# A gradient product on one core: all visits in a new order, and the last one split into 256 and 128 columns

## The chip, the core and the metric

The kernel runs on one core of a Trainium2 chip. A core has a matrix engine (TensorE, PE in the profile; its weight loads are shown apart, as PEld), VectorE (DVE), ScalarE (ACT), GpSimd (POOL) and SyncE (SP), each with its own queue of instructions, and 16 DMA engines which SP, ACT and POOL can give transfers to. Operands lie in SBUF, sums of TensorE in the eight banks of PSUM. The metric is the time of one execution on the device, in microseconds (us).

## What is computed

```python
# input: (16, 512, 1024) float32, grad_output: (16, 512, 768) float32
grad_weight = np.einsum('bmk,bmn->kn', input, grad_output)   # (1024, 768)
```

Batch and m are summed together: it is one product X^T G with X of 8192 x 1024 and G of 8192 x 768. The kernel rounds both to bf16 and sums in float32.

## The kernel before

**Blocks.** The output is cut into quarters: two halves of k (512 rows) by two halves of n (384 columns, LEFT and RIGHT). Each quarter has four row blocks q of 128. The quarters are called A (first k half, LEFT), B (first, RIGHT), C (second, LEFT), D (second, RIGHT). One matmul takes 128 rows of m as its contraction, 128 columns of X as weights, and 384 columns of G: every matmul is 128 by 128 by 384.

**Eight slabs plain, 28 pairs with seven products.** The first 1024 rows of m are eight slabs of 128 rows; each takes the four products A, B, C, D for every q. The other rows come as 28 pairs of 128 rows, each a 2 by 2 by 2 block product done with seven multiplications instead of eight (Winograd's form): streams A, B, C and 1, 5, 6, 7. Their operands are sums of halves of X and G, made by VectorE (`sum_x`, `sum_g`, lines 184 to 198, six instructions a pair). At the end the streams are joined: A gets 1, 6 gets 1, 7 gets 6, C gets 7, B gets 5, D is 5 minus 7, with D's own slabs folded in earlier (`SHARED`, and closings written with k). In all: 4 q x (3 x 36 + 8 + 4 x 28) = 912 matmuls.

**Visits.** There are 32 sums (8 streams x 4 q) and eight PSUM banks, so a sum visits a bank for a few matmuls, is evacuated to SBUF and comes back later. Three sums (A0, A1, A2) stay resident in banks 5 to 7 until near the end. Everything TensorE, VectorE, ScalarE and GpSimd do is written out as one list of tokens, `PLAN`, walked in order by the loop at the end of the function; each engine gets its instructions in exactly that order:

- `C0@2.1` opens bank 2 for C0 and does one matmul; `C0.1` goes on with one more; `@R` opens a resident bank (`multiply`, matmul at line 331).
- `fC2@0` has ScalarE copy C2's partial sum from SBUF into bank 0, so that the next visit adds onto it (`fill`, line 309; a trailing s takes it from an aside slot; two banks joined by + split it at column 256).
- `cC0` closes a visit by a ScalarE copy to SBUF (line 356), `vC0` by VectorE: a plain copy (line 376), an add onto the partial sum (378), or at the very end the join of two streams (364, 366, 371). `kC0` is the fold of D (360).
- `x0.4`, `g1.4` are VectorE's sums for pair 4. `r0` to `r4` are roundings of the first slabs to bf16: r0 is the RIGHT half of the first slab of G (VectorE), r1 and r2 halves of the second slab of X (VectorE), r3 and r4 the rest of it (ScalarE).
- `qA0` has GpSimd join two streams in SBUF (line 388) and stores the block; `pA3` joins ahead of the last visit ("prepared").

**Queues.** The first slabs come in float32 by SP and ACT (lines 128 to 131) and are rounded on chip; all other loads are cast to bf16 by GpSimd's DMA queue (lines 153 to 160), in order, into eleven buffers for pairs. Stores (line 291) go out on SP in the order of the tokens; the first HALVED of them are cut in two. Ahead of the first real matmul TensorE does 17 matmuls on constants, to the bank that A2 uses later (line 136).

Of the kernel before, what the change touches and what calls it, by code (L numbers as in the profile page):

```python
# [9 lines left out]
P = 128  # L10
# [4 lines left out]
    "C0@2.1 A0@R.1 r0 r1 r3 B1@1.1 r2 A2@R.1 r4 A1@R.1 vB1 A1.1 D3@4.2 A0.1 C0.1 D0@3.1 B2@0.1 cC0 B2.1 D0.1 "  # L15
    "fB1@1 A2.1 B3@2.2 cD3 B1.2 B3.1 D2@4.1 cB1 D2.1 vB3 D2.1 D0.1 A0.1 C1@2.3 C2@1.4 A1.2 cC2 B2.1 C1.1 B2.1 "
    "D2.1 cC1 D1@1.2 vD2 D1.1 fD3@2 D1.1 A2.2 cD0 vD1 B0@4.1 D3.2 A3@3.2 cD3 A3.2 B0.2 vA3 B0.1 C3@1.4 B2.2 "
    "B1@3.1 B0.1 cB2 B0.1 A1.2 cB0 D2@0.2 A0.3 D0@2.3 C3.2 A2.1 C0@4.1 vC3 C0.3 B1.2 B3@1.5 B1.1 D0.1 C0.1 vB1 "
    "C0.1 A0.2 vB3 D0.1 fD3@3 D2.2 vC0 fC3@1 A2.3 vD0 fD1@4 D3.3 vD2 D3.1 D1.1 g0.4 D1.1 fC1@0 D1.2 C3.1 fA3@2 "
    "g1.4 C3.1 C1.1 vD1 cD3 C1.3 kC3 fC2@3 A3.2 g2.4 A3.1 fB2@1 A3.1 x0.4 A3.1 C2.2 cA3 C2.1 x1.4 C2.2 A2.1 "  # L20
    "x2.4 10@2.1 cC2 A0.1 C1.1 v10 12@4.1 60@3.1 cC1 B2.1 g0.5 B2.1 c12 B2.1 61@0.1 g1.5 c60 62@2.1 B0@4.1 vB2 "
    "B0.1 c61 B0.1 11@3.1 c62 A1.1 vB0 A1.1 f12@1 A1.1 13@0.1 x0.5 13.1 12.1 11.1 c13 73@4.1 x1.5 73.1 c11 "
    "50@2.2 c12 k73 51@0.1 53@3.1 c50 53.1 x2.5 A1.1 52@4.1 g0.6 c53 52.1 51.1 fB1@2 A0.1 v52 63@1.2 c51 "
    "71@3.1 g1.6 71.1 fC0@4 g2.5 B1.2 g2.6 B1.1 c63 70@0.1 k71 70.1 C0.1 f10@1 C0.1 x0.6 C0.1 c70 B3@3.2 A1.1 "
    "cC0 10.1 x1.6 10.1 cB1 72@0.1 vB3 72.1 c10 72.1 C1@4.1 x2.6 f62@3 C1.1 60@2.1 k72 60.1 cC1 61@1.2 g0.7 "
    "A0.1 fB2@4 62.1 v61 62.1 B0@0.2 c62 g1.7 B2.2 vB0 c60 C3@1.2 cB2 C3.1 g2.7 C2@3.2 x0.7 fA3@2 C2.1 12@0.1 "
    "f51@4 12.1 vC3 A3.2 cC2 A3.1 v12 51.2 cA3 70@1.1 x1.7 70.1 c51 53@0.1 g0.8 53.1 A2.1 c70 A2.1 x2.7 A2.1 "
    "fB3@2 A1.1 v53 63@4.1 fB1@1 63.1 B3.1 g1.8 B3.1 f11@3 13@0.1 v63 13.1 cB3 B1.2 g2.8 11.1 v13 C3@4.1 cB1 "
    "C3.1 A2.1 x0.8 fC1@2s 11.2 C0@1.1 f71@0 C0.1 vC3 C1.2 cC0 71.1 x1.8 71.1 c11 71.1 vC1 52@1.2 c71 52.1 "
    "g0.9 A1.1 f73@3 60@4.2 v52 50@2.1 f62@0 50.1 g1.9 50.1 f13@1 73.1 v60 73.2 c50 62.1 x2.8 62.1 72@4.1 g2.9 "  # L30
    "72.1 c62 10@2.1 x0.9 10.1 c73 10.1 13.2 f70@0s v10 A0.2 f51@3 A0.1 v72 70.2 c13 51.1 x1.9 51.1 fC2@4s "
    "61@2.1 v70 61.1 fB2@1 61.1 C2.1 x2.9 C2.1 c51 B0@0.1 g0.10 B0.1 c61 B0.1 B2.1 vC2 B2.1 f11@3 B2.1 A2.1 "
    "vB0 f71@4 A3@2.2 x0.10 A3.1 cB2 11.1 A0.1 f12@0 11.1 g1.10 A2.1 71.1 f63@1 vA3 71.1 12.1 c11 12.1 g2.10 "
    "12.1 x1.10 c71 A1.2 g0.11 63.1 c12 63.2 fB1@4 x2.10 C1@3.2 g1.11 c63 62@2.2 vC1 B1.2 fB3@1 B1.1 v62 "
    "C0@0.1 fC3@3 C0.1 B3.1 g2.11 B3.1 cB1 B3.1 x0.11 C3.2 f72@4 C3.1 vC0 13@2.2 cC3 A2.1 x1.11 72.1 cB3 72.1 "
    "v13 72.1 f50@3s 73@0.2 g0.12 73.1 f53@1 52@2.2 v73 52.1 c72 50.2 g1.12 50.1 f60@0s 53.1 v52 53.1 fC0@4s "
    "53.2 g2.12 60.1 f51@2 v50 60.2 c53 A1.1 x0.12 A0.2 fB2@3 A1.1 C0.1 v60 f10@1 51.3 x1.12 C0.1 f70@0 10.2 "
    "vC0 c51 10.1 70.2 g0.13 70.1 f61@4s C2@2.2 x2.12 c70 C2.1 61.1 x2.11 c10 61.2 vC2 B2.2 f11@1 B2.1 g1.13 "
    "B0@0.1 f12@2 v61 B0.2 11.2 vB0 f62@4 11.1 12.2 cB2 x0.13 12.1 A3@0.1 c11 A3.2 g2.13 C1@3.1 f71@1 x1.13 "
    "C1.2 vA3 62.1 c12 62.2 g0.14 71.1 f63@0 71.2 x2.13 fC3@2 A2.1 63.1 vC1 63.1 c71 63.1 C3.1 g1.14 C3.1 c63 "  # L40
    "A2.1 g2.14 B3@1.1 c62 B3.2 x0.14 C3.1 A0.2 cC3 vB3 53@4.3 fB1@2 x1.14 73@0.2 v53 73.1 f72@1 50@3.2 x2.14 "
    "50.1 B1.1 v73 72.3 v50 60@4.2 c72 60.1 g0.15 B1.1 f52@0 B1.2 v60 13@3.3 A1.1 f70@4 x0.15 A1.2 cB1 52.2 "
    "v13 52.2 70.1 g1.15 70.1 c52 x1.15 70.1 A2.1 fC2@3 A2.1 g2.15 C0@0.1 g0.16 C0.1 c70 C0.1 C2.1 fB2@2 x2.15 "
    "C2.2 vC0 B0@4.2 cC2 B2.1 g1.16 B2.2 fC1@3 g2.16 51@1.2 vB0 51.1 cB2 12@0.2 x0.16 12.1 f10@4 C1.3 v51 10.2 "
    "cC1 10.1 x1.16 10.1 61@2.1 v12 61.1 c10 61.2 x2.16 f11@1 A1.1 71@0.1 g0.17 71.1 fB3@4 71.1 v61 62@3.3 v71 "
    "B3.3 v62 53@2.2 cB3 B1@0.1 g1.17 B1.1 11.1 v53 11.3 vB1 f60@2 A3@4.3 x0.17 c11 A3.1 A2.1 f72@3 A2.1 vA3 "
    "50@0.1 70@1.2 g0.18 72.1 f13@4 72.1 50.1 x1.17 50.1 72.1 v70 13.2 c72 13.1 g1.18 60.2 g2.17 c13 60.1 v50 "
    "63@1.1 fB2@3 63.2 g2.18 63.1 f73@0 A0.1 x0.18 A0.1 f52@4 A0.2 73.1 c60 x1.18 73.2 x2.17 73.1 52.1 x2.18 "
    "63.1 c73 C0@2.2 v63 C0.1 B0@0.2 vC0 B0.2 52.1 g0.19 52.1 fA3@2 A1.2 vB0 c52 B2.3 g1.19 f61@4 10@1.1 x0.19 "
    "10.2 A3.2 g2.19 51@0.2 x1.19 cA3 51.2 v10 cB2 A2.1 61.2 f62@2 v51 61.1 C1@3.2 x2.19 fC2@0 C1.1 62.1 g0.20 "  # L50
    "62.2 B1@1.1 vC1 B1.1 c62 C2.1 g1.20 B1.1 f53@3 A2.1 A1.1 g2.20 12@2.1 c61 vB1 12.3 f11@4 x0.20 C2.2 f70@1 "
    "C2.1 53.1 v12 53.1 cC2 53.2 x1.20 11.2 v53 A2.1 70.1 c11 70.1 x2.20 70.1 fB0@3 52@2.1 g0.21 52.1 B2@0.1 "
    "c70 B2.1 B3@4.1 g1.21 B3.1 v52 B3.2 B0.1 vB2 B0.1 C3@1.2 g2.21 C3.1 fC2@0 C3.1 vB3 C3.1 cB0 C3.2 A0.1 "
    "f72@2 A0.1 vC3 A0.1 13@4.1 C2.1 x0.21 13.1 f50@1 13.2 71@3.1 g0.22 71.2 x1.21 71.2 g1.22 72.3 g2.22 72.1 "
    "v71 50.2 c72 50.2 C2.1 x0.22 fC1@2 C2.1 13.1 A1.1 f60@3 A1.1 x1.22 A1.1 cC2 C1.2 v13 c50 C1.1 60.1 x2.21 "
    "60.1 cC1 60.1 x2.22 60.1 f63@0 60.1 C0@1.2 v60 C0.2 63.1 g0.23 63.3 vC0 A0.1 B0@3.1 c63 B0.1 g1.23 61@4.1 "
    "f51@1 61.2 x0.23 62@0.1 f11@2 62.1 51.1 vB0 51.3 x1.23 11.2 v61 11.2 61@3.1 A0.1 A2.1 v61 A2.2 62.1 v11 "
    "62.1 73@4.2 g0.24 f70@2 73.3 x2.23 c51 10@3.2 v62 10.1 fA3@1 10.2 x0.24 A1.2 70.2 x1.24 70.2 v10 50@0.3 "
    "x2.24 A3.2 v50 A3.3 v73 B1@3.1 fB3@0 B1.2 g2.23 cA3 B1.1 g0.25 B1.1 c70 B3.2 vB1 B3.1 f13@1 B3.1 12@2.1 "
    "g1.25 f53@4 12.2 x0.25 12.1 f52@3 12.1 53.2 vB3 53.2 x1.25 53.1 13.2 v12 13.1 52.1 g1.24 52.1 c13 52.1 "  # L60
    "g2.25 52.1 c53 52.1 x2.25 63@2.1 A0.1 f11@0 g0.26 63.2 B2@1.1 g1.26 11.2 v63 A2.2 B2.2 f60@2 x0.26 B2.2 "
    "c11 A0.1 B0@4.1 c52 B0.1 x1.26 B0.1 60.1 g2.24 fC2@0 60.1 g2.26 60.2 71@3.2 g0.27 c60 71.1 C2.2 x2.26 "
    "C2.2 vB0 C3@2.1 B2.1 A1.1 g1.27 fC0@4 A1.1 kC2 C3.3 g2.27 C3.1 f72@0 C0.2 x0.27 C0.3 vC3 71.3 kC0 72.1 "
    "fC1@2 72.2 vB2 72.1 fA3@4 72.2 x1.27 C1.2 c72 v71 C1.3 g0.28 f73@0 62@1.3 fB3@3 kC1 62.1 A0.1 73.1 g1.28 "
    "73.1 f51@2 v62 73.2 A3.1 g2.28 A3.2 x0.28 A3.1 52@1.2 cA3 51.1 x2.27 51.1 c73 51.1 x1.28 51.2 52.1 A1.1 "
    "50@0.1 v52 50.3 v51 61@4.1 f70@1 61.2 g0.29 61.2 70.1 g1.29 70.2 v61 70.1 A2.1 A1.1 v50 B3.1 f63@4 12@2.2 "
    "x0.29 12.1 63.3 x1.29 A2.2 g2.29 A2.1 70.1 x2.28 63.1 A0.1 v12 A0.2 B3.1 k70 B3.2 B1@0.1 x2.29 B1.1 cB3 "
    "B1.1 g0.30 B1.1 c63 B1.1 10@2.2 x0.30 f60@4 10.4 vB1 60.2 53@3.1 g1.30 53.2 x1.30 53.2 g2.30 13@0.2 v53 "
    "13.2 60.2 g0.31 f72@3 A1.2 f11@1 v10 A0.1 A2.1 72.1 g1.31 72.1 f12@2 72.1 11.1 g2.31 11.1 x2.30 11.2 "
    "x0.31 11.2 A1.1 13.1 c11 13.1 x1.31 12.1 cA1 12.1 v13 12.1 A0.1 f62@1 A2.1 x2.31 10@6.1 p63 c12 72.1 60.1 "  # L70
    "v10 cA2 62.3 cA0 62.1 v60 63@7.1 f73@6 63.1 qA0 v62 A3@0.1 f70@4 A3.1 73.1 v63 73.1 f50@5 73.2 qA2 v72 "
    "70.1 f53@2 A3.1 50.1 v73 70.1 fC3@3 53.1 50.1 v70 f61@1 qA1 50.1 C3.2 v53 fC2@7 C3.2 fB3@6 C3.1 pA3 61.2 "
    "cC3 61.1 v50 C2.1 f71@4 C2.3 qC3 f51@3 C2.1 v61 71.2 cC2 71.1 vA3 71.1 fC0@1 B3.1 qC2 B3.1 v71 B3.1 fB1@7 "
    "51.2 vB3 f52@0 51.1 C0.1 pC1 C0.1 fB0@4 v51 C0.2 fB2@5 C1@2.4 vC0 B1.2 52.1 vC1 52.2 vB1 B2.3 v52 B2.2 "
    "B0.4 vB2 B0.2 vB0 "
).split()

WARMUP = [("b", 512), ("f", 512), ("f", 512)] + 14 * [("b", 128)]
PAIRS_HELD = 11
SUMS_HELD = 8  # L80
MERGED = 2
HALVED = 4
ASIDES = 7
# [5 lines left out]
def kernel(  # L89
# [6 lines left out]
    nc = tc.nc  # L96
    bf16 = mybir.dt.bfloat16
    f32 = mybir.dt.float32
# [242 lines left out]
    def close(engine, p, q, queue):  # L341
# [39 lines left out]
        if last(p, q) and not opened[p, q] and not (engine == "c" and p in "ABC"):  # L381
            closed.add((p, q))
# [66 lines left out]
```

## Time and profile before

| | |
|---|---|
| time, median of 3 runs | 161.19 us (161.19 to 161.51) |
| the profiled execution's own time | 161.48 us |
| its span in the profile | 159.7 us |
| TensorE clock granted | 0.999 of full speed |
| matmuls of the product | 912 |
| first and last of them start | 5.91 and 155.75 us |
| last VectorE instruction | 156.12 to 156.68 us |
| last store issued | 156.70 us |

The profile is that of one execution. A busy time counts the stretch from an instruction's start to its end; matmuls overlap, so that a matmul row shows about 326 ns for one while the next starts after half of that, and short waits between two matmuls can't be seen in the busy time: they are read from the starts. In rows of the timeline the columns are the start, the length, engine, line, operation, what it writes and reads, its shape, how many were merged into the row, and in brackets the idle time before it and who ended it. The chain of waits follows the work that ended last back to the start. A DMA's time to landing goes from its issue to the semaphore that reports it.

### The profile page before, as it was taken

The numbers are of one execution on the slowest core, as the hardware profiler recorded it, in microseconds if no ns is written. First come the engines' busy times: TensorE is split into PE (matmuls) and PEld (weight loads), VectorE is DVE, ScalarE is ACT, GpSimd is POOL, SyncE is SP. The second block draws the span as 40 slices with busy tenths as digits, with TensorE's granted clock in tenths as the row PEclk, the third lists the DMA queues.
The fourth block names the chain that finished last, engine by engine and source line by source line (L and its number), as shares of the span: only waits on it lengthen the run. The fifth ranks groups of instructions, "written<-read, shape, count | busy, mean of one in ns | idle before, by whom it ended". The sixth has DMA issues, their size and how long they took to land.

```text
span 159.7 us, 2734 instructions
## 1 busy us (share of the span) xinstructions
PE 154.6 (97%) x931; PEld 91.2 (57%) x931; DVE 136.1 (85%) x316; ACT 104.4 (65%) x243; POOL 42.6 (27%) x77
## 2 busy tenths in 40 slices
PE   8899999999999999999999999999999999999990
PEld 3456656556555565665656565656566565656560
DVE  0514169999999999999999999989999899999992
ACT  3445238999999999967867585563465472339930
POOL 7442222222212222221222221222222100006930
PEclk9999999999999999999999999999999999999999
DMA  5999999999999999999999999999999999940696
GB/s 171 297 212 211 214 216 212 213 213 212 213 213 211 214 212 213 214 211 214 213 214 212 214 213 214 212 211 213 213 211 219 208 214 213 213 81 0 196 353 239
DMA packets 12829, 33.40 MB, mean 209 GB/s; under 512 B 1424, under 2 KB 4624, under 8 KB 12816
## 3 DMA queue, kind: packets, MB, share of 16 engines
q0 software_dynamic: 9360, 28.64, 90.7%
q1 hardware_dynamic: 3168, 3.54, 6.6%
q10 hardware_dynamic: 288, 1.05, 1.7%
q8 instruction: 7, 0.11, 0.3%
q14 instruction: 6, 0.05, 0.1%
HBM read 58.72 MB, written 3.15 MB: 387 GB/s over the span
## 4 chain that ended last, share of the span: by engine, by line
PE 91%; DMA 4%; DVE 2%; issue 1%; ACT 0%; ACTq 0%; DVEq 0%
PE bank L331 91%; DMA xf<-in_input_dram 4%; DVE acc L371 1%; DVE macc L364 0%; DVE xp L202 0%; ACT macc L356 0%; ACTq L129 0%; DVE acc L378 0%; DVE acc L366 0%; DVEq L371 0%
## 5 line engine op out<-in xcount | busy, mean ns | idle before, releaser
L331 PE MATMUL bank<-gp,xp 128*128 128x384 bf16 x576 | 105.4, 326 | 0.7 <-DVE xp L202 0.6
L331 PEld LDWEIGHTS <-xp 128*128 128x128 bf16 x576 | 55.8, 98 | 39.1 <-DVE xp L202 1.0
L331 PE MATMUL bank<-ge,xe 128*128 128x384 bf16 x336 | 65.9, 326 | 0.0
L331 PEld LDWEIGHTS <-xe 128*128 128x128 bf16 x336 | 32.7, 98 | 22.3 <-DVE xe L184 0.6
L309 ACT COPY bank<-macc 128x384 f32<-128x384 f32 x69 | 32.6, 489 | 10.4 <-DVE macc L378 6.2
L356 ACT COPY macc<-bank 128x384 f32<-128x384 f32 x64 | 29.4, 484 | 10.4 <-PE bank L331 10.1
L378 DVE TENSOR_TENSOR macc<-bank,macc 128x384 f32<-128x384 f32 x56 | 30.5, 554 | 1.2 <-PE bank L331 0.9
L154 POOL DMA_DIRECT2D xp<-in_input_dram x30 | 15.9, 529 | 52.6 <-DMA xp<-in_input_dram 21.9
L309 ACT COPY bank<-acc 128x384 f32<-128x384 f32 x46 | 21.8, 485 | 11.5 <-DVE acc L378 8.9
L356 ACT COPY acc<-bank 128x384 f32<-128x384 f32 x44 | 20.7, 480 | 11.4 <-PE bank L331 11.1
L153 POOL DMA_DIRECT2D gp<-in_grad_output_dram x30 | 15.9, 531 | 38.4 <-PE bank L331 17.2
L378 DVE TENSOR_TENSOR acc<-bank,acc 128x384 f32<-128x384 f32 x42 | 22.8, 553 | 1.9 <-PE bank L331 1.9
L184 DVE TENSOR_TENSOR xe<-xp 128x1024 bf16<-128x1024 bf16 x28 | 19.3, 689 | 1.0 <-DMA xp<-in_input_dram 0.9
L194 DVE TENSOR_TENSOR ge<-gp 128x768 bf16<-128x768 bf16 x28 | 15.5, 552 | 0.2 <-DMA gp<-in_grad_output_dram 0.2
L376 DVE COPY acc<-bank 128x384 f32<-128x384 f32 x9 | 5.0, 555 | 8.9 <-PE bank L331 8.9
L186 DVE TENSOR_TENSOR xe<-xe,xp 128x512 bf16<-128x512 bf16 x28 | 11.8, 421 | 0.3
L188 DVE TENSOR_TENSOR xp<-xp,xe 128x512 bf16<-128x512 bf16 x28 | 11.5, 419 | 0.0
L196 DVE TENSOR_TENSOR ge<-gp,ge 128x384 bf16<-128x384 bf16 x28 | 9.9, 353 | 0.2
L198 DVE TENSOR_TENSOR gp<-ge,gp 128x384 bf16<-128x384 bf16 x28 | 9.8, 354 | 0.2
L388 POOL TENSOR_TENSOR acc<-acc,macc 128x384 f32<-128x384 f32 x7 | 6.8, 1003 | 0.5 <-ACT acc L356 0.5
L388 POOL TENSOR_TENSOR macc<-macc 128x384 f32<-128x384 f32 x1 | 1.0, 1042 | 18.0 <-DVE macc L378 18.0
L202 DVE CAST gp<-gf 128x192 bf16<-128x192 f32 (+1 forms) x2 | 0.6, 310 | 4.9 <-DMA gf<-in_grad_output_dram 4.9
(23 smaller groups left out, 41.2 us busy)
## 6 DMA issues: line engine op xcount, KB each, us to landing
xp<-in_input_dram POOLq DMA_DIRECT2D x30, 512.0 KB, 16.7
gp<-in_grad_output_dram POOLq DMA_DIRECT2D x30, 384.0 KB, 16.7
out_dram<-acc SPq DMA_DIRECT2D x12, 192.0 KB, 2.1
xf<-in_input_dram ACTq DMA_DIRECT2D x2, 512.0 KB, 4.9
out_dram<-acc SPq DMA_DIRECT2D x8, 96.0 KB, 1.7
gp<-in_grad_output_dram POOLq DMA_DIRECT2D x3, 192.0 KB, 6.4
xp<-in_input_dram POOLq DMA_DIRECT2D x2, 256.0 KB, 7.8
gf<-in_grad_output_dram SPq DMA_DIRECT2D x2, 192.0 KB, 4.1
```

The lines of the kernel that those rows point to most:

```text
L153: nc.gpsimd.dma_start(out=gp, in_=G[rows, :].rearrange("(p m) n -> p m n", m=2))
L154: nc.gpsimd.dma_start(out=xp, in_=X[rows, :].rearrange("(p m) k -> p m k", m=2))
L184: nc.vector.tensor_sub(out=xe[:, 0:2, :], in0=x[:, 1::-1, :], in1=x[:, 3::-2, :])
L186: nc.vector.tensor_sub(out=xe[:, 2, :], in0=xe[:, 0, :], in1=x[:, 0, :])
L188: nc.vector.tensor_add(out=x[:, 1, :], in0=x[:, 2, :], in1=xe[:, 2, :])
L194: nc.vector.tensor_add(out=ge[:, 0:2, :], in0=g[:, 0:2, :], in1=g[:, 1::2, :])
L196: nc.vector.tensor_add(out=ge[:, 2, :], in0=g[:, 3, :], in1=ge[:, 0, :])
L198: nc.vector.tensor_add(out=g[:, 1, :], in0=ge[:, 2, :], in1=g[:, 2, :])
L309: nc.scalar.copy(out=tile_[:, at : at + c1 - c0], in_=src[:, c0:c1])
L331: nc.tensor.matmul(tile_[:, at : at + c1 - c0], stat, mov[:, c0:c1], start=fresh, stop=True, skip_group_check=True,)
L356: nc.scalar.copy(out=to, in_=b)
L378: nc.vector.tensor_add(out=to, in0=b, in1=to)
```

## The change

All tokens of the plan are in a new order: other blocks go first, other banks are used, other engines close some visits. The number of matmuls is the same. At the end the last visit, of B2, is filled into two banks, 256 columns in bank 7 and 128 in bank 1, and its matmuls are done twice, first the 256 columns for all of them, then the 128. The existing code for a join of two parts then adds and stores each part by itself, the first on SP, the second on ScalarE's queue. Three stores are halved in place of four. The first warm-up matmul writes bank 4, the other 16 bank 7. A closing by ScalarE may now also be the last of a prepared block. The load of the second slab of X can be cut, which `X1_PARTS = 1` leaves off.

The plan's beginning and end, and the rest of the diff:

```diff
 PLAN = (
-    "C0@2.1 A0@R.1 r0 r1 r3 B1@1.1 r2 A2@R.1 r4 A1@R.1 vB1 A1.1 D3@4.2 A0.1 C0.1 D0@3.1 B2@0.1 cC0 B2.1 D0.1 "
+    "A0@R.1 C2@2.1 A3@3.1 A2@R.1 cC2 A1@R.1 vA3 C0@1.1 C1@0.1 vC1 r3 r0 r2 D2@4.1 r1 D2.1 vC0 B0@2.2 B1@0.2 "
+    "cB0 D1@1.2 r4 C3@3.3 D2.1 A1.1 cC3 A1.1 vD2 A2.1 cB1 A2.1 B3@2.2 fC1@0 B3.1 C0@3.2 fA3@4 C1.2 vC0 C1.1 "
...
-    "51.2 vB3 f52@0 51.1 C0.1 pC1 C0.1 fB0@4 v51 C0.2 fB2@5 C1@2.4 vC0 B1.2 52.1 vC1 52.2 vB1 B2.3 v52 B2.2 "
-    "B0.4 vB2 B0.2 vB0 "
+    "61.1 qA2 61.1 v70 50.1 cA0 50.2 f52@0 v61 53.1 72.1 fB3@7 72.1 qC0 v50 72.2 fC3@3 52.2 B3.1 f71@5 "
+    "B3.1 v72 qA0 C3.1 fC2@2 C3.2 v53 C3.1 cB3 C3.1 71.1 f51@4 71.1 qB3 71.1 v52 cC3 71.2 C2.1 fB2@7+1 C2.2 "
+    "qC3 C2.1 v71 C2.1 fC1@0 51.2 vC2 fB1@3 51.1 C1.2 v51 fB0@6 C1.2 B1.2 B0.2 vB1 B0.3 vC1 B0.1 B2.2 vB0 B2.5 "
+    "vB2 "
 ).split()
 
-WARMUP = [("b", 512), ("f", 512), ("f", 512)] + 14 * [("b", 128)]
+WARMUP = [("b",512),("f",512),("f",512)]+14*[("b",128)]
-HALVED = 4
+X1_PARTS = 1
+HALVED = 3
...
-    nc.scalar.dma_start(out=xf[1], in_=X[P : 2 * P, :])
-
-    wps = psum.tile([P, 512], f32, name="bank7")
-    for dt, cols in WARMUP:
+    if X1_PARTS == 1:
+        nc.scalar.dma_start(out=xf[1], in_=X[P : 2 * P, :])
+    else:
...
+    warm = [psum.tile([P, 512], f32, name=f"bank{b}") for b in (4, 7)]
+    for n, (dt, cols) in enumerate(WARMUP):
...
-            wps[:, 0:cols],
+            warm[min(n, 1)][:, 0:cols],
...
                 assert not final or p in "ABC"
+                assert (p, q) not in prepared or (final and carried and len(parts) == 1)
                 nc.scalar.copy(out=to, in_=b)
...
-        if last(p, q) and not opened[p, q] and not (engine == "c" and p in "ABC"):
+        if final and engine == "c" and (p, q) in prepared:
+            store(p, q, 0, NH, queue)
+        if last(p, q) and not opened[p, q] and (engine != "c" or p not in "ABC" or (p, q) in prepared):
             closed.add((p, q))
```

## The prediction

> **What bounds it now.** I read the page first, then the chain of waits, then the timeline at both ends, then the busy time by windows. The page and its chain:
>
> ```profile
> span 159.7 us, 2734 instructions
> PE 154.6 (97%) x931; PEld 91.2 (57%) x931; DVE 136.1 (85%) x316; ACT 104.4 (65%) x243; POOL 42.6 (27%) x77
> ...
> PE 91%; DMA 4%; DVE 2%; issue 1%; ACT 0%; ACTq 0%; DVEq 0%
> ```
>
> TensorE is 91% of the chain. Its pace comes from a row of the tail, `154.13 1.95 ... x11` below: less the 0.33 of the last one, ten steps take 1.62 us, 0.1625 each. The 912 matmuls start at 5.91 (first) and 155.75 (last): 149.84 us for 911 steps worth 148.04. So 1.80 us is waiting, and that, with what stands behind the last matmul, is all the change can win. The start:
>
> ```profile
> 5.91 1.17 PE L331 MATMUL bank<-gp,xp 128*128 128x384 bf16 x5
> 6.02 0.36 DVE L202 CAST gp<-gf 128x384 bf16<-128x384 f32 x1 [0.71 <-DMA gf<-in_grad_output_dram]
> ...
> 7.14 0.50 DVE L202 CAST xp<-xf 128x256 bf16<-128x256 f32 x2 [0.76 <-DMA xf<-in_input_dram]
> 7.14 0.71 ACT L202 CAST xp<-xf 128x256 bf16<-128x256 f32 x2 [1.73 <-DMA xf<-in_input_dram]
> 7.55 0.55 DVE L376 COPY acc<-bank 128x384 f32<-128x384 f32 x1
> ...
> 7.70 7.49 PE L331 MATMUL bank<-gp,xp 128*128 128x384 bf16 x45 [0.62 <-DVE xp L202]
> ```
>
> Five matmuls need only the first slabs; the sixth waits for `xf[1]` (landed 7.12) and its rounding. They take 1.79 us instead of 0.81: 0.98 of the 1.80. The other 0.82 is spread: in the starts of single matmuls 0.05 at 30.2, 0.15 at 40.4 (a VectorE closing), 0.12 at 51.8 (a load of input), 0.25 at 88.9 (a ScalarE closing), 0.16 at 126.5 (sums of a pair whose input landed at 125.71, some 0.6 off the even rhythm of the landings), 0.09 in crumbs. The end:
>
> ```profile
> 154.13 1.95 PE L331 MATMUL bank<-gp,xp 128*128 128x384 bf16 x11
> ...
> 155.55 1.13 DVE L371 TENSOR_TENSOR acc<-bank,macc 128x384 f32<-128x384 f32 x2
> ```
>
> ```profile
> 156.70 0.33 SPq L291 DMA_DIRECT2D out_dram<-acc  x1
> ```
>
> ```profile
> out_dram<-acc SPq DMA_DIRECT2D x12, 192.0 KB, 2.1
> ...
> out_dram<-acc SPq DMA_DIRECT2D x8, 96.0 KB, 1.7
> ```
>
> Call T the start of the last matmul (155.75). It ends at T+0.33, the last add runs from T+0.36 to T+0.92, its store is issued at T+0.95 and lands at T+3.04 (158.80); 0.87 of ending follows.
>
> **The start, part by part.** Both kernels' first matmul follows the warm-up (last 128-column one at 5.85), which keeps its 17 instructions; that the first writes bank 4 I put at nothing: nothing else touches bank 4 until matmul 8, on the same engine. Bounds: 0 to the 0.16 of one step. After the change seven matmuls come first: A0 C2 A3 A2 A1 C0 C1, all on the left columns, so the wait for the right columns at the third matmul (0.20) goes. At 0.1625 each they start from 5.91 to 6.89. What is late next: D2 needs the right columns, and their rounding (r0) now stands on VectorE behind vA3 and vC1. C1 ends at 6.89+0.33=7.21; vC1 starts at 7.25; VectorE's next instruction starts 0.465 later (adds in a row in the tail start at 155.09 and 155.55), so r0 runs from 7.71 to 8.07 (0.36), and matmul 8 starts at 8.11. Queued behind it on VectorE are r2 (7.99) and r1 (8.20), needed at 8.60 and 9.25; r3 on ScalarE has run at 7.14. In before matmul 8 starts at 8.03. Cost **+0.08**; with no copy ahead of r0 it would be −0.6, with one more ahead +0.55.
>
> **The middle.** Counted in the plans: VectorE's evacuations 141 and 140 (one in two pieces), ScalarE's closings 115 and 119, its fills 122 and 124 (one in two), pair sums the same 168, GpSimd's adds 8 and 8. Nothing is saved; the order counts. VectorE is nearly full:
>
> ```profile
> 32.00:38.00 6.00, 6.00 (x38) 3.53 (x37) 5.91 (x15) 5.83 (x15) 1.58 (x3) 1.00 1.06 210
> 38.00:44.00 6.00, 6.00 (x38) 3.48 (x36) 5.90 (x15) 5.78 (x15) 1.58 (x3) 1.00 1.08 215
> 44.00:50.00 6.00, 6.00 (x39) 3.62 (x37) 6.00 (x16) 5.82 (x15) 1.22 (x3) 1.00 1.07 214
> ```
>
> (columns: stretch, its length, then busy time and count of PE, PEld, DVE, ACT, POOL, then clock, DMA share, GB/s). With the distances between starts of VectorE instructions in a row (0.465 a closing, 2.26 the six sums of a pair) matmuls 152 to 912 carry 117.1 us of VectorE work in before and 114.7 in after, against 123.5 of TensorE: the new order does 2.4 us more of it early, where VectorE is half idle. The heaviest stretch (matmuls 190 to 342, 24.7 of TensorE) goes the other way, 24.3 to 24.6. Loads stay: DMA is full to 142 us (share 1.07), and buffers are freed long before they are refilled. Against the landings of before the new order has no reserve at matmuls 30 (wants 11.85, landed 11.88), 83 and 275 (51.75): 0.07+0.01+0.05=0.13 of waits that no order of queues removes. The waits of before that hang on the engines' queues (0.05+0.15+0.25+0.09=0.54) I take down to 0.38, since VectorE has less to catch up; the late landing at 126.5 meets a place where the sums are wanted 16 matmuls later. So 0.82 becomes 0.51: **−0.31**. Bounds: 0.13 (−0.69) and, all queue waits twice as long, 1.2 (+0.4).
>
> **The last visit.** 7 steps of 384 columns become 7 of 256 and 7 of 128. (The new branch for a ScalarE closing of a prepared block issues nothing: A3 and 62, the only prepared ones, are closed by VectorE; the second form of the input load is switched off.) The warm-up shows 128 columns at full clock:
>
> ```profile
> 5.74 0.34 PE L136 MATMUL bank<-const-bfloat16-1.0 128*128 128x128 bf16 x3
> ```
>
> (0.34−0.22)/2=0.06 a step; 256 columns lie between 0.06 and 0.1625, by the line through both 0.11. Seven pairs: 7·0.17=1.18 for 1.14, **+0.04**. The weights are loaded 14 times: a load takes 0.098 in the page's PEld rows, longer than 0.06, yet the three warm-up steps carry one each at 0.06. The Trainium skill ("TensorE: Matmul & The Clock Gate", section Back-to-back issue gap) gives 81 ns for 128 columns in a stream of load and matmul pairs, against 56 alone; by it the visit would cost 0.16 more, and the trace's 0.06 is nearer to its second figure.
>
> Now T' is the start of the last 128-column matmul, T' = T+0.14 for the same start of the visit. The last 256-column one starts at T'−0.34 and ends at T'−0.07; its add starts at T'−0.03. No row has an add this narrow: the 384-column one takes 0.55 and holds VectorE 0.465, so 256 columns are between 0.29 (a 256-column cast) and 0.55, by columns 0.42; 128 between 0.23 and 0.55, by columns 0.28. First add to T'+0.39, second T'+0.30 to T'+0.58. Stores: SP at T'+0.42, ScalarE's queue at T'+0.61. The 64 KB one lands after 1.6 (shortest store of the trace) to 2.1; I take the middle, 1.85. Landing T'+2.46 = T+2.60 instead of T+3.04: **−0.44**, from −0.2 to −0.7. It needs VectorE free: in the new tail v51, vB1, vC1, vB0 follow matmuls 892, 898, 903, 904, at 0.465 each, done 0.4 before. And SP free: it issues about every 0.49; three halvings instead of four spare it one issue of 0.4, so that it is free some 0.05 ahead of the last one. With four, the last would be 0.35 late. Tightest: fC1@0 waits for v52, 15 VectorE instructions in a row after v63; 0.1 in hand.
>
> **Sum.** Own time of the profiled execution 161.48: +0.08 −0.31 −0.44 = 160.81. It lies 0.29 above the median 161.19; on the median's scale 160.52. Part of the 0.29 may be that late landing, 0.16, which a median run would not have to lose: I say **160.6**, with 160.2 to 160.9 for this case.
>
> **Rivals.**
> 1. TensorE waits for landings alone (0.13): another −0.38, about 160.1. For it: VectorE's 2.4 us. Against: queue waits in before at places with no heavy load. 0.15.
> 2. Nothing moves in the middle and the small store takes the full 2.1: −0.2+0.08, about 161.1. For it: the six-us windows are full in either order. 0.19.
> 3. The 128-column steps go at the pace of the weight loads, 0.098: 7·0.04=0.28 on top, 160.9. For it: 14 loads in a row onto two banks, which the warm-up (one bank, one constant) doesn't show. 0.05.
> 4. Slower: turnover of banks closed and refilled by ScalarE. Last matmul 0.33, close 0.41 to the next instruction, fill 0.49, signals 0.08: 1.3 us. In after nine such banks are reopened 11 steps (1.79) after their last matmul, in before nine at 13 (2.11). With two other ScalarE instructions (0.8) ahead, each costs 0.3. Four of nine hit: 1.2−0.44+0.08−0.30 (before's own waits on ScalarE, at 30.2 and 88.9, in exchange), about 161.7; it decides from three on. Against: 13 banks of before at 10 to 12 steps left only that 0.30. 0.18.
>
> Forecast 0.43. Faster than 0.2% (0.32 us, about what can be told from none): forecast and rival 1 with a little of rival 2, 0.60; rivals 2 and 3, 0.22; slower 0.18. The range goes from a little under rival 1 to a little over rival 4, whose fifth bank is left out: 159.9 to 161.9.
>
> **What would show it.** Seven matmuls by 7.2, the eighth at 8.1 behind the cast of the right columns; last matmul 0.3 us earlier in its place; 128-column steps of 0.06; two last stores, ScalarE's landing about 2.5 after the last matmul starts. Wrong if a wait over 0.3 stands before a matmul whose bank ScalarE refilled, or if the narrow store takes 2.1.

## The result, and the profile after

| | before | after |
|---|---|---|
| median of 20 runs each | 161.38 us (161.17 to 161.73) | 161.57 us (161.35 to 161.83) |
| ratio of the times | | 1.0014, 95% interval 1.0008 to 1.0021 |
| the profiled execution: time, span | 161.48, 159.7 | 161.56, 159.6 |
| last matmul starts | 155.75 | 155.41 |
| last store issued, landed | 156.70, 158.80 | 156.11, 158.66 |

The change costs 0.19 us: by the bound of 0.2% it is no difference, by its own interval a small loss. The forecast was 160.6, a gain; the range held the time. (The 161.19 that the forecast started from was the median of three runs; that of twenty is 161.38.) The page:

```profile
span 159.6 us, 2750 instructions
PE 153.7 (96%) x938; PEld 91.2 (57%) x938; DVE 136.6 (86%) x316; ACT 107.6 (67%) x250; POOL 42.6 (27%) x77
...
PE 91%; DMA 4%; POOL 1%; issue 0%; DVE 0%; DVEq 0%; POOLq 0%
```

TensorE's share of the chain is still 91%. What stands ahead of it is the load of the third slab of X; in before it was the load of the second slab and its rounding. The pieces of the chain in order of time (start, length, what):

```profile
2.47 7.15 DMA xp<-in_input_dram
9.62 0.05 issue
9.66 145.70 PE bank L338 x897
155.37 0.03 issue
155.39 0.43 DVE acc L379
155.82 0.20 DVEq L454
```

From the landing of the third slab of X at 9.62, TensorE runs 145.70 us for 897 matmuls with no wait long enough to make a piece of its own. (This view ends with the last engine; the stores' landings after it have to be read from the DMA's rows.) The start, in the timeline of TensorE:

```profile
4.82 0.69 PE L143 MATMUL bank<-const-bfloat16-1.0 128*128 128x128 bf16 x9
5.35 1.36 PE L338 MATMUL bank<-gp,xp 128*128 128x384 bf16 x7
7.63 1.78 PE L338 MATMUL bank<-gp,xp 128*128 128x384 bf16 x10 [0.91 <-DVE gp L209]
9.66 2.54 PE L338 MATMUL bank<-gp,xp 128*128 128x384 bf16 x14 [0.25 <-DMA xp<-in_input_dram]
```

Seven matmuls, then the wait for the cast of the right columns (`gp`), as forecast; then, ten matmuls on, a second wait that the forecast did not have. And the end:

```profile
155.39 0.62 DVE L379 TENSOR_TENSOR acc<-bank,macc 128x256 f32<-128x256 f32 x2 [0.25 <-PE bank L338]
156.04 0.37 ACTq L298 DMA_DIRECT2D out_dram<-acc  x1
```

Both adds are done by 156.01, where before's last one ended at 156.68. Yet the last store lands only 0.14 earlier than before's. The rows of the DMA issues, with the median time from issue to landing last, say why:

```profile
out_dram<-acc SPq DMA_DIRECT2D x12, 192.0 KB, 2.2
...
out_dram<-acc SPq DMA_DIRECT2D x6, 96.0 KB, 1.7
...
out_dram<-acc SPq DMA_DIRECT2D x1, 128.0 KB, 2.5
out_dram<-acc ACTq DMA_DIRECT2D x1, 64.0 KB, 2.3
```

The 64 KB and the 128 KB take longer than 192 KB do. They are not the slower for being small; they are last in a line. Busy time by windows, after (the last two columns are the DMA engines' busy share and GB/s):

```profile
148.00:151.50 3.50, 3.50 (x23) 2.13 (x22) 3.50 (x9) 3.50 (x10) 3.10 (x4) 1.00 0.64 209
151.50:158.00 6.50, 4.13 (x33) 2.72 (x30) 4.26 (x10) 1.59 (x5) 1.07 (x2) 1.00 1.02 362
```

and before:

```profile
152.00:158.30 6.30, 4.08 (x26) 2.25 (x23) 4.65 (x10) 1.11 (x3) 1.11 (x2) 1.00 1.02 366
```

For the last 6.5 us the 16 DMA engines are full with stores: one block of 192 KB needs 0.54 us at 362 GB/s. After's last ten blocks become ready between 151.61 and 156.01, one for each 0.49 us, and SP issues one for each 0.49. So the stores fall behind a little with each block, and their latencies grow from 2.10 for the store issued at 151.65 to 2.55 for the last (the first halves, in a quiet stretch, took 1.63). In the 3.5 us ahead of that the engines are only 0.64 busy. In part that is the halved stores, which give SP 96 KB for each 0.49 us of issuing; without halves (e1 below) the share there is 0.73, and the rest is blocks that are not ready yet.

A last difference lies outside the span. Time less span is 1.78 in the mean of before's runs (those beside the experiments) and **1.96** in after's. The trace of after has one transfer that before's has not: an 8 KB fetch of instructions at 161.29, 1.7 us after the span's end.

### The profile page after: what moved, and what is told of

It is laid out like the page before. It is cut to its first block, busy times and chain, and to the rows that moved or that the text cites. A ratio compares the mean times of both kernels' runs of the same rounds, so it can differ in the third digit from the quotient of the medians.

```text
span 159.6 us, 2750 instructions
## 1 busy us (share of the span) xinstructions
PE 153.7 (96%) x938; PEld 91.2 (57%) x938; DVE 136.6 (86%) x316; ACT 107.6 (67%) x250; POOL 42.6 (27%) x77
## 4 chain that ended last, share of the span: by engine, by line
PE 91%; DMA 4%; POOL 1%; issue 0%; DVE 0%; DVEq 0%; POOLq 0%
PE bank L338 91%; DMA xp<-in_input_dram 4%; POOL gp L165 1%; DVE acc L379 0%; DVEq L454 0%; POOLq L443 0%
## 5 line engine op out<-in xcount | busy, mean ns | idle before, releaser
L338 PE MATMUL bank<-gp,xp 128*128 128x384 bf16 (+2 forms) x583 | 104.8, 324 | 1.2 <-DVE gp L209 0.9
L338 PE MATMUL bank<-ge,xe 128*128 128x384 bf16 x336 | 64.9, 326 | 0.0
L316 ACT COPY bank<-macc 128x384 f32<-128x384 f32 x66 | 31.3, 488 | 11.1 <-DVE macc L386 6.8
L364 ACT COPY macc<-bank 128x384 f32<-128x384 f32 x62 | 28.8, 484 | 7.8 <-PE bank L338 7.5
L386 DVE TENSOR_TENSOR macc<-bank,macc 128x384 f32<-128x384 f32 x59 | 32.1, 552 | 1.2 <-PE bank L338 0.8
L316 ACT COPY bank<-acc 128x384 f32<-128x384 f32 (+2 forms) x52 | 24.5, 482 | 12.6 <-DVE macc L386 7.1
L364 ACT COPY acc<-bank 128x384 f32<-128x384 f32 x50 | 23.3, 482 | 10.3 <-PE bank L338 10.2
L386 DVE TENSOR_TENSOR acc<-bank,acc 128x384 f32<-128x384 f32 x40 | 21.8, 552 | 7.5 <-PE bank L338 7.3
L384 DVE COPY acc<-bank 128x384 f32<-128x384 f32 x8 | 4.4, 554 | 3.4 <-PE bank L338 3.3
L379 DVE TENSOR_TENSOR macc<-bank,macc 128x384 f32<-128x384 f32 x7 | 3.7, 551 | 0.0
```

Source lines behind the costliest of these rows:

```text
L316: nc.scalar.copy(out=tile_[:, at : at + c1 - c0], in_=src[:, c0:c1])
L338: nc.tensor.matmul(tile_[:, at : at + c1 - c0], stat, mov[:, c0:c1], start=fresh, stop=True, skip_group_check=True,)
L364: nc.scalar.copy(out=to, in_=b)
L386: nc.vector.tensor_add(out=to, in0=b, in1=to)
```

## The experiments

Theory A said at first that the three halved stores cost the gain. Its form A1 puts it to SP's pace of issuing, its form A2 to the DMA engines' draining. Rival B puts the loss to the split of the last visit. C, that the time outside the span comes from the late instruction fetch, was formed from the first runs; E, on the list of waits that ends SP's program, from the second. In the table, "time" and "span" are means of a run's kernel less the means of before, run beside it on the same chip, and "outside" is its time less its span (before: 1.77 to 1.79). One of the 35 runs of before that stand beside e1 to e4 took 163.21; without it, time and span of these four rows would be 0.05 higher.

| run | time | span | outside |
|---|---|---|---|
| e1_halved0 | +0.15 | −0.01 | 1.94 |
| e2_unsplit | −0.05 | −0.06 | 1.79 |
| e3_two_queues | +0.03 | +0.03 | 1.78 |
| e4_before_halved0 | +0.31 | +0.32 | 1.76 |
| e5_warm_one_bank | +0.21 | +0.03 | 1.96 |
| e6_fewer_bytes | +1.94 | +1.84 | 1.87 |
| e7_before_fewer_bytes | +2.25 | +2.22 | 1.81 |
| e8_four_more_on_act | −0.11 | −0.11 | 1.77 |
| e9_narrow | −0.42 | −0.59 | 1.94 |
| e10_before_narrow | −0.28 | −0.29 | 1.78 |
| e11_all | −0.13 | −0.15 | 1.79 |
| e12_halved0_count | −0.03 | −0.25 | 1.99 |
| e13_before_halved0_count | +0.16 | +0.17 | 1.78 |
| e14_unsplit_count | −0.26 | −0.25 | 1.79 |
| e15_count_mid | +0.02 | +0.03 | 1.78 |

**e1_halved0**: the changed kernel, no store halved.

```diff
-HALVED = 3
+HALVED = 0
```

> The changed kernel with no store halved. In its profile TensorE's last matmul starts 0.34 us earlier than in before, but the last store lands only 0.14 earlier (158.66 for 158.80), and from 151.5 to 158 the 16 DMA engines are full with stores (183 KB each 0.5 us), after a stretch at 100 KB each 0.5 us in which SP sends halves. Theory A, the row of stores sets the end (SP sends one each 0.49 us whatever its size, then the DMA engines drain 368 GB/s): without halves the first three blocks go in three issues in place of six, some 1.2 us less of issuing; the last stores go as soon as their data is there (155.84 and 156.04) and land after about 1.7 in place of 2.55 and 2.34: the time falls by 0.6 to 1.0 us. Theory B, the two small stores of the split are slow in themselves (512-byte and 1-KB rows, two queues): they still need 2.3 to 2.5, and only SP's wait goes: 0 to 0.25 us.

Measured 161.67, ratio to before 1.0006 (0.9986 to 1.0025).

```profile
148.00:151.50 3.50, 3.50 (x24) 2.08 (x22) 3.50 (x9) 3.50 (x10) 3.10 (x4) 1.00 0.73 261
```

SP now waited for blocks up to 151.73. From there on it issued one for each 0.49 us as in after, the last at 156.10, and the last two stores still took 2.23 and 2.37. The last landing came only 0.16 earlier than in after (158.49), and the end of the span not at all. Theory A's forecast of 0.6 to 1.0 failed.

**e2_unsplit**: the changed kernel, last visit in one bank.

```diff
-    ... cC3 71.2 C2.1 fB2@7+1 C2.2 "
+    ... cC3 71.2 C2.1 fB2@7 C2.2 "
```

> The changed kernel with the last visit of B2 in one bank again: 7 matmuls of 384 columns, one add, one store of 192 KB on SP. Theory A (row of stores): the data is ready at about 156.2 in place of 156.0, SP is free at 156.1, and the DMA engines are full until 158.3 either way: no change, -0.05 to +0.15 us. Theory B (the small stores are slow): their last landing 2.55 after issue becomes 2.1 as in before: 0.2 to 0.4 us faster. Also read here: the part of the time that lies outside the span, 1.81 us in the profiled execution of before and 1.96 on average in the changed kernel's runs; if the store on ScalarE's queue made it longer, it is back at 1.8 here.

161.43, ratio 0.9994 (0.9975 to 1.0013). The span is that of after within 0.1: the split gains nothing. Its store goes out at 156.48 where the split ones go at 156.04 and 156.11, takes 2.32, and lands at 158.80, 0.14 later. The time is 0.14 under after's for another reason: outside 1.79, and no fetch after the end. B, which expected 0.2 to 0.4, came near the time, but not by its cause: the whole store is as late as the small ones.

**e3_two_queues**: the changed kernel, two of the last stores moved from SP to ScalarE's queue.

```diff
-    ... fB0@6 C1.2 B1.2 B0.2 vB1 B0.3 vC1 B0.1 B2.2 vB0 B2.5 "
+    ... fB0@6 C1.2 B1.2 B0.2 vB1a B0.3 vC1 B0.1 B2.2 vB0a B2.5 "
```

> The changed kernel with the stores of B1 and B0, the ones ahead of the last, sent on ScalarE's queue, which has no more fills by then. Theory A comes in two forms. A1, SP's pace of issue binds: SP is free when the last store's data is there, so it goes 0.27 us earlier, and so does the end: -0.2 to -0.3 us. A2, the DMA engines' drain binds: the stores go out earlier and land no earlier: -0.05 to +0.05 us. Theory B: no change, or slower by 0.1 with one more store on the slower queue.

161.53, ratio 1.0 (0.9981 to 1.0019).

```profile
153.74 2.54 SPq L298 DMA_DIRECT2D out_dram<-acc  x4
...
154.29 2.20 ACTq L298 DMA_DIRECT2D out_dram<-acc  x3
```

Two queues issue side by side, and SP's last issue comes at 155.95 instead of 156.11. But the landings are at 158.66 and 158.82, with latencies up to 3.08. What is issued sooner waits longer: A2, not A1. This agrees with the Trainium skill ("DMA: Bandwidth & Descriptors", section Issuing engines are not separate DMA queues), by which transfers of all issuers share the same 16 engines and a second issuer saves issuing time alone. The fetch moved too, to 160.41, 0.7 after the span's end; outside fell to 1.78.

**e4_before_halved0**: before, no store halved.

```diff
-HALVED = 4
+HALVED = 0
```

> The kernel before, with no store halved. There the last store's data is ready at 156.68, after SP is free, so that only the backlog of the DMA engines can be won. Theory A: the last store lands after about 1.7 in place of 2.1 us: 0.2 to 0.4 us faster than before. Theory B: no change, within 0.1 us. If e1 wins more than this one, the earlier end of TensorE in the changed kernel is real and was hidden by the stores.

161.83, ratio 1.0018 (0.9998 to 1.0039): 0.3 longer, against the expectation. The profiled execution was the shortest of its runs (161.45), since its last matmul starts 0.37 earlier than before's. Counted from that matmul its end is 0.34 later: the last store takes 2.19 in place of 2.10, and from its landing to the end of the span 1.16 us pass in place of 0.91; see e12 and e13.

**e6_fewer_bytes** and **e7_before_fewer_bytes**: the first 13 blocks stored from 64 partitions, in after and in before; the kernel leaves the other half of these blocks out of the output.

```diff
-            engine.dma_start(out=OUT[:, row, at + d0 : at + d1], in_=sum_of(p, q)[:, d0:d1])
+            top = P // 2 if stores[0] <= 13 else P
+            engine.dma_start(out=OUT[0:top, row, at + d0 : at + d1], in_=sum_of(p, q)[0:top, d0:d1])
```

> The changed kernel with the first 13 of the 16 blocks stored from 64 partitions in place of 128: half their bytes are left out of the output, everything else is done. Theory A2, left over from the first four runs: the DMA engines drain the stores at 368 GB/s from 151.5 on, and the blocks become ready faster than that (ten in the last 4.4 us, 0.52 each to drain), so that neither SP's pace nor the last block's readiness (156.01) sets the end. With half the bytes there is no backlog: the last issue stays at about 156.1 (SP's pace) and lands after about 1.7 in place of 2.55, at 157.8 in place of 158.66: 0.7 to 0.9 us faster. Rival B, the small stores or the end of the program set it: within 0.1 us of the changed kernel.

> The kernel before with the same bytes left out. Theory A2: its last data is ready at 156.68, and a 192 KB store without backlog lands after about 1.9 (first stores of the run without halves) in place of 2.10: 0.1 to 0.3 us faster than before. The difference to the run on the changed kernel, 0.5 to 0.7 us, is then what the earlier end of TensorE and the split would have been worth with a free row of stores. Rival B: no change, within 0.1 us.

163.43, ratio 1.0119 (1.0106 to 1.0133), and 163.75, ratio 1.0139 (1.0126 to 1.0152): both far slower, and no test of A2, since the edit brought a bound of its own. SP's stores in e6 (duration in ns: shortest, median, longest):

```profile
L299 SPq DMA_DIRECT2D out_dram<-acc x19: 393/549/603, 147.3 to 158.7; - x19
```

In after the median is 402. A store from 64 partitions costs SP 0.55 to issue where one from 128 costs 0.40; SP issues until 158.7 and the DMA engines are 0.59 busy from 151.5 to 156. The bytes were halved in the wrong dimension.

**e8_four_more_on_act**: the changed kernel with four 128 by 1 copies on ScalarE ahead of the plan (and a small memset on VectorE).

```diff
+    spare = accp.tile([P, 8], f32, name="spare")
+    nc.vector.memset(spare, 0.0)
+    for b in range(4):
+        nc.scalar.copy(out=spare[:, 4 + b : 5 + b], in_=spare[:, b : b + 1])
     for token in PLAN:
```

> The changed kernel with four one-column copies more on ScalarE (and a memset on VectorE) near the start, where both wait. The trace of the changed kernel has one 8 KB fetch of instructions at 161.29, after the span; the one without halves has it at 161.36; before and the unsplit one have none, and in the run with two more stores on ScalarE's queue it lies at 160.41. The part of the time outside the span is 1.95 us in the first two and 1.78 in the others. Theory C, the fetch is that of ScalarE's instructions, which reach over the end of a block of 8 KB by a little, and it holds up the end of the execution by 0.17 us: with four more instructions it comes earlier, the part outside the span is 1.78, and the time falls by 0.15 to 0.2 us. Rival D, the part outside goes with something else (the stores' queues): it stays at 1.95, and the time is the changed kernel's.

161.37, ratio 0.9993 (0.9984 to 1.0001). Four more instructions, and the time is 0.2 shorter than after's: the 8 KB fetch now falls at 160.31, 0.5 after the span's end, and outside is 1.77, as theory C expects. (The span is also 0.14 shorter than that of e5, run beside it, which C does not give and nothing here explains.) Over all runs the fetch 1.7 after the end goes with 1.94 to 1.99 outside (after, e1, e5, e9, e12), the fetch 0.5 to 0.7 after it, or none, with 1.76 to 1.79 (e6 and e7 aside). It follows the count of ScalarE's instructions in the trace: none with 304 or 313, 1.7 after the end with 316, 0.5 to 0.7 after it with 320. Since e3 moves it with VectorE and TensorE untouched, I take it for ScalarE's stream. That the fetch itself holds up the end is not shown apart from this count.

**e5_warm_one_bank**: the changed kernel, all warm-up matmuls on bank 7.

```diff
-    warm = [psum.tile([P, 512], f32, name=f"bank{b}") for b in (4, 7)]
+    warm = [psum.tile([P, 512], f32, name=f"bank{b}") for b in (7, 7)]
```

> The changed kernel with all 17 warm-up matmuls in bank 7, as in before. Every theory so far: no change, within 0.1 us of the changed kernel; the first matmul of the product starts between 5.2 and 6.1 in the traces of either kind of warm-up, with the moment at which the clock is granted, and the loads that bound matmuls 17 and 30 land at the same times. If the two banks bring something, this one is slower by more than 0.1.

161.69, ratio 1.0013 (1.0004 to 1.0022), against after's 1.0014: the second bank brings nothing that shows.

**e9_narrow** and **e10_before_narrow**: the first 13 blocks are stored with half their columns, on all 128 partitions, in after and in before; the other half is left out of the output.

```diff
+            d1 = (d0 + d1) // 2 if stores[0] <= 13 else d1
             engine.dma_start(out=OUT[:, row, at + d0 : at + d1], in_=sum_of(p, q)[:, d0:d1])
```

> The changed kernel, of whose first 13 stores only the left half of the columns is written (half the bytes are left out of the output, all 128 partitions, the same number of stores). The run from 64 partitions failed to separate: SP then needed 0.64 us for an issue and became the bound itself. Theory A2 (drain of the DMA engines, full from 151.5 on): without a backlog the last two stores go at 155.9 and 156.05 and land after about 1.7: 157.7 in place of 158.66, 0.7 to 0.9 us faster than the changed kernel. Rival B (small stores or program end): within 0.1 us.

> The kernel before with the same columns left out. Theory A2: last data ready at 156.68, landing 1.9 after issue in place of 2.10: 0.1 to 0.3 us faster than before. Against the run on the changed kernel this gives the worth of the change with a free row of stores: that one should be 0.4 to 0.6 faster than this one, in spite of its 0.17 outside the span. Rival B: no change.

160.96, ratio 0.9972 (0.9962 to 0.9982), and 161.11, ratio 0.9983 (0.9974 to 0.9992). In e9:

```profile
151.50:156.00 4.50, 4.10 (x33) 2.72 (x30) 4.24 (x10) 1.57 (x5) 1.04 (x2) 1.00 0.65 209
156.00:158.00 2.00, 0.00 (x0) 0.00 (x0) 0.00 (x0) 0.00 (x0) 0.00 (x0) 1.00 0.79 267
```

With the line of stores gone (DMA 0.65 busy until 156) the last stores take 1.89 (128 KB) and 1.99 (64 KB) and land at 157.79 and 158.01. The forecast had taken 1.85 for the 64 KB. The span falls by 0.59. Before gains 0.29 by the same edit, so that e9's span ends 0.30 under e10's: this much the split and the new order are worth where the DMA has room. Of it the late fetch, which e9 still has, takes back 0.17 in the time. A2 is shown, at 0.6 and not at the 0.7 to 0.9 it expected: the last three blocks, which keep all their columns, still fill the engines from 156 to 157 (share 1.02), and their stores took 1.9 to 2.0 and not 1.7.

**e12_halved0_count**: e1 with three loads of 256 bytes more on SP at the start.

```diff
-HALVED = 3
+HALVED = 0
...
+    few = accp.tile([1, 192], f32, name="few")
+    for b in range(3):
+        nc.sync.dma_start(out=few[:, 64 * b : 64 * (b + 1)], in_=G[0:1, 64 * b : 64 * (b + 1)])
```

> The changed kernel with no store halved, and three loads of 256 bytes each on SP near the start, which nobody uses, so that the number of SP's and ScalarE's DMAs is 24 as in the changed kernel. Theory E, from the ends of the first four traces: at the end SP waits for eight DMA semaphores in a fixed order, 0.06 us for one that has long fired; they are dealt out in turn, so with 24 DMAs the last store's comes last, with 21 (no halves) three more waits follow it, and 0.24 us passes between its landing and the end of the list. With 24 again, this run is 0.15 to 0.25 us faster than the one without halves, and 0.1 to 0.25 faster than the changed kernel, since its stores drain a little earlier (last landing 158.49 for 158.66, though TensorE had ended 0.08 later). Rival F: stores without halves cost time in another way (they did in before: 0.3 us): no better than the run without halves.

161.34, ratio 1.0001 (0.9992 to 1.001); its span is 0.24 under that of e1, though it does more. SP's instructions in the trace end with eight waits, one on each of the semaphores that the transfers of SP and ScalarE use in turn. They stand in a fixed order, 0.06 us each even where the transfer has long landed. In e1, with 21 such transfers, the wait for the last landing (158.49) ends at 158.51, and four more waits stand behind it, to 158.78. In e12, with 24, the last landing's wait is the list's last: landed 158.376, passed 158.39. (e2, with 23, has one wait behind its last landing.) Before and after both have 24, 20 stores and 4 loads: the split ending adds a store, and three halvings in place of four keep the count. Theory E holds; it is why the span of e1 showed nothing of the 0.16 that its stores gained.

**e11_all**: e12 with the four copies of e8.

```diff
-HALVED = 3
+HALVED = 0
...
+    for b in range(3):
+        nc.sync.dma_start(out=few[:, 64 * b : 64 * (b + 1)], in_=G[0:1, 64 * b : 64 * (b + 1)])
...
+    for b in range(4):
+        nc.scalar.copy(out=spare[:, 4 + b : 5 + b], in_=spare[:, b : b + 1])
```

> The last one with the four small copies on ScalarE too, which moved the late fetch of instructions. Theories C and E together: the changed kernel less 0.17 outside the span and 0.1 to 0.25 at the end, 161.15 to 161.3 where the changed kernel has 161.57; that would be 0.1 to 0.3 us under before. Rival F: 161.4, the run with the four copies alone.

161.28, ratio 0.9995 (0.9984 to 1.0006): outside is 1.79 again, but the span is 0.10 longer than e12's. In its trace ScalarE's store lands last (158.34) and SP's wait for the other stands behind it, 0.06 of this; the rest is open, as the copies did not lengthen e8's span. Not told from before.

**e13_before_halved0_count**: before, no store halved, four loads of 256 bytes more on SP (24 transfers).

```diff
-HALVED = 4
+HALVED = 0
...
+    few = accp.tile([1, 256], f32, name="few")
+    for b in range(4):
+        nc.sync.dma_start(out=few[:, 64 * b : 64 * (b + 1)], in_=G[0:1, 64 * b : 64 * (b + 1)])
```

> The kernel before with no store halved took 161.83, 0.3 longer than with four halved, though its stores are fewer. Here four more 256-byte loads stand on SP's queue at the start, so that it has 24 DMAs again, as before has. Theory E (the waits at the end of the list, dealt by the count of DMAs modulo eight, 0.06 each): the waits behind the last store's go, 161.83 - 0.25 = 161.6 or a little less. Rival (the stall of whole stores lies in the middle, where buffers or the DMA engines are held longer): no change, 161.7 to 161.9.

161.53, ratio 1.001 (1.0002 to 1.0019). Against its own before +0.16, where e4 had +0.31: the list of waits explains half of e4's loss by these means, though the two intervals overlap and the runs were on two chips. In e13's trace the time from the last landing to the end is back at 0.90, and the last store takes 2.19 as in e4, 0.09 more than before's. The rest of the 0.16, and why whole stores leave a longer line in before, stay open.

**e14_unsplit_count**: the changed kernel, unsplit, no store halved, the four loads (24 transfers).

```diff
-    ... cC3 71.2 C2.1 fB2@7+1 C2.2 "
+    ... cC3 71.2 C2.1 fB2@7 C2.2 "
...
-HALVED = 3
+HALVED = 0
...
+    few = accp.tile([1, 256], f32, name="few")
+    for b in range(4):
+        nc.sync.dma_start(out=few[:, 64 * b : 64 * (b + 1)], in_=G[0:1, 64 * b : 64 * (b + 1)])
```

> The changed kernel with the last visit unsplit (no late fetch, 0.17 saved outside the span), with no store halved and four more 256-byte loads on SP at the start (24 DMAs: the last store's wait is the last of the list, 0.25 saved at the end of the span). Theory E and the fetch together: the unsplit kernel's 161.43 less 0.2 to 0.3, 161.15 to 161.25, and 0.15 to 0.25 under the kernel before. Rival (what the whole stores save is lost again in the unsplit ending, whose last store is 192 KB on a full DMA): 161.4 to 161.5.

**161.07**, ratio 0.9985 (0.9976 to 0.9994): under both kernels, by 0.3 and by 0.5 (after's 161.57 by way of before, whose median was 161.38 both times).

```profile
out_dram<-acc SPq DMA_DIRECT2D x16, 192.0 KB, 2.0
```

All 16 stores are whole, and their median is 2.0 where that of after's whole ones was 2.2: the engines move 298 GB/s from 150.0 to 151.5 where after's move 228, so less is left for the end. The last one takes 2.08 and lands at 158.40, though it is issued 0.2 later than after's. Against e2, the same kernel with three halved stores, the span is 0.19 shorter (0.24 without the run of 163.21); 0.06 of that is the one wait less at the end of SP's list.

**e15_count_mid**: e12 with the four copies within the plan (at tokens 150, 170, 190 and 210).

```diff
-    for token in PLAN:
+    for at, token in enumerate(PLAN):
+        if at in (150, 170, 190, 210):
+            b = (at - 150) // 20
+            nc.scalar.copy(out=spare[:, 4 + b : 5 + b], in_=spare[:, b : b + 1])
```

> The changed kernel with no store halved, three 256-byte loads on SP at the start (24 DMAs), and four 128x1 ScalarE copies in the first third of the plan (not at its start, where the run of that form had a span 0.1 longer). If the fetch behind the span's end goes by the number of ScalarE's instructions: outside of the span 1.78 again, and with the span of 159.39 of the form without copies 161.15 to 161.2. If the copies cost span wherever they stand: 161.25 to 161.3.

161.41, ratio 1.0001 (0.9992 to 1.001). The fetch is gone from behind the end (160.22, outside 1.78), but the span is 0.28 longer against its before than e12's, which ran on another chip: a miss.

```profile
35.84 0.57 ACT L320 COPY bank<-macc 128x384 f32<-128x384 f32 x1
36.25 0.56 ACT L368 COPY macc<-bank 128x384 f32<-128x384 f32 x1
```

At 36.07 TensorE waits 0.13 for a ScalarE closing (line 368) of that stretch, at 32.37 and 37.25 another 0.06 together; the copies stand where ScalarE is full. These waits were absent in e12 there. As in e11, ScalarE's store lands last and one wait more stands behind it, 0.06. The rest of the 0.28 is not accounted for: its first matmul was 0.2 later in the profile, and that moment varies, as told below under the start.

## Why the prediction was wrong, point by point

- **The start** (+0.08): right in kind, and of no weight. Matmul 8 starts behind the cast r0, which ran at 7.23 behind vC1, as forecast; but at 7.63 and not 8.11, since the warm-up ended 0.56 sooner in this execution: all its 128-column steps take 0.06, while before's take 0.107 until 5.6. In the traces of these kernels the first matmul comes anywhere from 5.2 to 6.1, with either plan. Of the 0.48 only 0.07 is left ten matmuls on: matmul 18 needs the third slab of X, landed at 9.62, and starts at 9.66; from the forecast 8.11 it would have been 9.73. The landing holds what the start varies.
- **The middle** (−0.31): right in kind, and under-sized in this execution. Rival 1's condition came true: behind matmul 18 TensorE waits for landings alone, at 11.87, 20.50, 90.58, 94.89 and 142.60; these add up to 0.28, where the forecast left 0.51. In the profiled executions the last matmul starts 0.34 earlier than before's; over all traces (five of before's plan, twelve of after's) the last matmul ends at 155.93 and 155.72 in the mean, −0.21, where the forecast's terms (+0.08 −0.31 +0.04) gave −0.19. Single executions scatter by 0.4 to 0.5, so the agreement is in part luck. Rival 4, the turnover of ScalarE's banks, does not show in after.
- **The last visit** (+0.04): right. The 256-column steps take 0.109, the 128-column ones 0.056, with a weight load of 0.098 each, so that the loads overlap one another; rival 3 is out, and the 81 ns of the Trainium skill ("TensorE: Matmul & The Clock Gate", section Back-to-back issue gap) is not borne out in these rows. (The visit is written as two tokens, so the 256 columns are not done for all seven first: two of 256 and two of 128 come first, then five and five.) The adds took 0.43 and 0.28, forecast 0.42 and 0.28.
- **The last stores: the step that failed.** The forecast said "The 64 KB one lands after 1.6 (shortest store of the trace) to 2.1; I take the middle, 1.85. Landing T'+2.46 = T+2.60 instead of T+3.04: **−0.44**". The 64 KB were issued at T'+0.63 (forecast 0.61) and took 2.34; the 128 KB were issued at T'+0.69 (forecast 0.42, SP was not free) and took 2.55. The landing came at T'+3.24, 0.78 late. That three halvings leave SP free was wrong as well: SP issued the 128 KB 0.29 after their data was ready. I took latencies as a property of a store's size, from medians over stores of which some stood in no line. The DMA row of before's page shows the engines busy in its last slices; read by windows, it would have shown 1.02 from 152.0 to 158.3, and that the last landing follows from the bytes. In e9, where half the bytes of the earlier stores are gone, the last landing comes at T'+2.62, 0.16 behind the forecast in place of 0.78; e3 shows that sooner issues don't help. And the forecast set a quiet latency, 1.85, against before's landing at T+3.04, whose store stood in a line itself: with room its 2.10 becomes 1.89 (e10). So with room the change is worth 0.30 of span (e9 against e10), not the 0.67 of the sum.
- **What the sum did not have**: the 0.18 outside the span. The sum took time less span as a constant of 1.78; after against e2, e3 and e8 shows that it is not one. (The ending from the last landing to the end of the span, 0.87 in the forecast, is 0.91 in both traces.)

Put together: what TensorE ends sooner, about 0.2, is lost in the line of stores, so that the span ends as before's does (after, e2, e3, e5 and e8, all with after's order and halves, lie −0.11 to +0.08 from before's, the run of 163.21 left out), and the time outside it, 0.18 longer where the late fetch stands, makes nearly all of the +0.19. "Wrong if the narrow store takes 2.1" was the right place to look, for the wrong reason. Rival 2 had the right end of that range (2.1), at 161.1; the store went past it.

## What to carry to other kernels

Before an ending is split to store sooner, add up the bytes that still have to leave and read the DMA share of the last microseconds: where it is full, the last landing is set by the drain, and splitting the last store gains nothing (e2). What did gain with this order was to send the earlier stores whole (e12, e14); in the kernel before, whole stores lost (e4, e13), so that this has to be tried. Latencies read from a quiet stretch hold for a quiet stretch. And on differences of 0.1%, look outside the span and at the program's tail too, where a few instructions or transfers more or less moved 0.2 us that no step of the kernel accounts for.

## What the runs showed of the hardware

- The list of waits at the end of SP's program: 0.06 us each in a fixed order, so that the count of SP's and ScalarE's transfers, modulo eight, moves the end by up to 0.25 (from the last landing to the end of the span: 0.91 with 24 transfers, or 0.97 where ScalarE's store lands last, 0.97 with 23, 1.15 with 21, 1.16 with 20; e1 to e12: −0.24 of span).
- An 8 KB instruction fetch 1.7 us after the span's end goes with 0.17 to 0.2 us more outside the span; one 0.5 after it with nothing more (after and e8).
- A store from 64 partitions holds SP 0.55 us, one from 128 partitions 0.40 (medians of e6 and after).
- In the stretch in which SP sends halves, one of 96 KB for each 0.49 us, the DMA engines are 0.64 busy at 209 GB/s (after, 148.0 to 151.5); with whole stores, not all of them ready in time, 0.73 and 261 (e1). One whole store for each 0.49 us fills them, at 362 (after, 151.5 to 158).
